# Values matmuls of latent attention: once per head pair over wide rows, with kept transposed probabilities

## Chip, cores and metric

The kernel runs on one NeuronCore of a Trainium2 chip. The metric is the device time of one execution in microseconds (us). The engines are named as in the profile: PE is TensorE's matmul stream and PEld its weight loads, DVE is VectorE, ACT is ScalarE, POOL is GpSimd and SP is SyncE.

## What is computed

Two residual layers over x of shape (1, 512, 1024) in float32. Layer 0 mixes with SSD and GLA heads, layer 1 with multi-head latent attention, and a SwiGLU FFN follows each. The change touches only layer 1's attention: 16 heads of width 64 + 32 (rotary), values of width 64, a causal softmax over 512 tokens in blocks of 128 queries.

```python
def block(i):
    start = i * ATTN_BLOCK
    ...
    s = jnp.einsum('bqhd,bkhd->bhqk', qn, k_nope) + jnp.einsum('bqhr,bkr->bhqk', qr, k_rope)
    s = s.astype(jnp.float32) * scale
    ...
    p = jax.nn.softmax(jnp.where(mask, s, -jnp.inf), axis=-1).astype(v.dtype)
    return jnp.einsum('bhqk,bkhv->bqhv', p, v)
o = lax.map(block, jnp.arange(seqlen // ATTN_BLOCK))
...
return o @ w_o
```

## The kernel before

Everything is one TensorE program in a framework that takes the instructions in program order, gives each engine its own in-order queue, and lets an instruction that comes later in the program go first at compile time when an earlier one's inputs are not expected to be ready. So the program order is a priority, and an engine at run time executes its queue strictly in the order that came out.

Dense layers hold each operand as two parts of a reduced-width type; `mm3` (lines 141 to 143) does three matmuls of 512 columns for each pair of chunks and accumulates into one of three PSUM banks named `acc`. `weight` (lines 135 and 136) loads a weight and splits it on ACT and DVE, 90 instructions ahead of its place.

Layer 1 works on groups of four heads and on pairs of heads. `project(g)` computes q, k and v of a group, token-major. `prepare(g, hp, ...)` transposes keys and queries of a pair: 4 transposes at line 821 and 8 at line 834, into the key tiles `kT` (6 of them, `NK`) and the query tiles `qT` (4). `attend(g, hp, ...)` then goes through the four query blocks b, and in each through the two heads j:

- line 848: the scores of 128 queries against (b+1) x 128 keys, into one of two PSUM banks `sco`
- line 852 (DVE): scale, mask and row minimum into `sc` (6 buffers, `SC`)
- line 854 (ACT): exp with the row sum, then line 856 (DVE) the reciprocal and line 857 (DVE) the normalisation
- line 861 (PE): b+1 transposes of 128 x 128 into one of two PSUM banks `ptr`, and line 863 (ACT) the copy into `pt` (4 buffers of 512 columns, `PT`)
- line 867 (PE): after both heads, for each key block kb up to b and each head, a matmul of 128 columns with the 64 value columns of the head as weights. Head 0 writes partitions 0 to 63 of the bank `po`, head 1 writes 64 to 127

After the four blocks `split` (lines 120 and 121) takes `po` to two parts. The main loop runs `prepare` of the next pair ahead of `attend` of this one. `project(2)` comes after pair 0, `project(3)` after pair 2, and `o_round(0)`, the dense product of the first four pairs with half of w_o, after pair 4. `o_round(1)` comes after pair 7. These dense products are what PE can do while a pair's softmax is on its way.

Of the kernel before, what the change touches and what calls it, by code (L numbers as in the profile page):

```python
# [8 lines left out]
F32 = mybir.dt.float32  # L9
F32R = mybir.dt.float32r  # L10
I32 = mybir.dt.int32
AF = mybir.ActivationFunctionType
ALU = mybir.AluOpType
# [13 lines left out]
SC, PT = 6, 4  # L27
# [4 lines left out]
# columns of the packed per-partition vectors  # L32
# [13 lines left out]
def kernel(ctx: ExitStack, tc: tile.TileContext, A, yT, stop=99):  # L46
# [11 lines left out]
    def nm(s):  # L58
        cnt[0] += 1
        return f"{s}_{cnt[0]}"  # L60
# [6 lines left out]
    def open_phase(**tags):  # L67
        """the other banks, by role"""
        if phase:
            phase["pool"].__exit__(None, None, None)  # L70
        phase["pool"] = tc.tile_pool(name=nm("pph"), bufs=1, space=PSUM)
        phase["p"] = phase["pool"].__enter__()
        phase["tags"] = tags
# [26 lines left out]
    # sel[:, c]: row 32 c is one  # L100
# [4 lines left out]
    # tri[s, l] = 1 where s <= l  # L105
# [10 lines left out]
    def split(raw_ap, th, tl, bufs, pool):  # L116
        """raw float32 [128, 512] -> exact parts hi + lo, both float32r"""
        hi = pool.tile([P, T], F32R, tag=th, name=nm(th), bufs=bufs)
        lo = pool.tile([P, T], F32R, tag=tl, name=nm(tl), bufs=bufs)
        S.copy(hi, raw_ap)  # L120
        V.tensor_tensor(lo, raw_ap, hi.bitcast(F32), ALU.subtract)
        return hi, lo

    def weight(src, kc, m):
        """src: DRAM AP [128, kc, m]; loaded and split ahead of what comes before it here"""
        with tc.high_priority(offset=AHEAD):
            return weight_now(src, kc, m)
# [17 lines left out]
    def dense(ps, w, xs):  # L145
        """ps[m, t] = sum over the chunks of w (stationary) and xs [(hi, lo)]"""
        n = len(xs)
        for k, (xh, xl) in enumerate(xs):
            mm3(ps, w[0][:, k, :], w[1][:, k, :], xh, xl, k == 0, k == n - 1)

    def rsqrt(pool, m, shape, tag, ytag=""):
        """1/sqrt(m) by bit estimate and three Newton steps; m > 0"""
        h = pool.tile(shape, I32, tag=tag + "i", name=nm(tag + "i"), bufs=1)
        y = pool.tile(shape, F32, tag=tag + ytag + "y", name=nm(tag + "y"), bufs=1)
        t = pool.tile(shape, F32, tag=tag + "t", name=nm(tag + "t"), bufs=1)
        V.tensor_scalar(h, m.bitcast(I32), 1, None, ALU.logical_shift_right)
        V.tensor_scalar(y.bitcast(I32), h, -1.0, float(0x5F3759DF), ALU.mult, ALU.add)
        for _ in range(3):
            V.tensor_tensor(t, y, y, ALU.mult)
            V.scalar_tensor_tensor(t, m, -0.5, t, ALU.mult, ALU.mult)  # L160
            V.scalar_tensor_tensor(y, t, 1.5, y, ALU.add, ALU.mult)
        return y

    def rstd(ssq, n, pool, tag):
        """ssq [128, 512]: partial sums of squares -> R [128, 512], 1/rms on every partition"""
        ps = aux()
        for c in range(4):
            E.matmul(ps[32 * c:32 * c + 32, :P], ones, ssq[:, c * P:(c + 1) * P],
                     start=True, stop=True)
        m = const.tile([P, P], F32, tag="rs_m", name=nm("rs_m"))  # L170
        V.tensor_scalar(m, ps[:, :P], 1.0 / n, EPS, ALU.mult, ALU.add)
        y = rsqrt(const, m, [P, P], "rs")
        pb = aux()
        for c in range(4):
            E.matmul(pb[:, c * P:(c + 1) * P], sel[:, c, :], y, start=True, stop=True)  # L175
        R = pool.tile([P, T], F32, tag=tag, name=nm(tag), bufs=1)
        S.copy(R, pb)
        return R

    class Norm:  # L180
        """collects the chunks of the residual: squares, and x * gain in two parts"""
# [26 lines left out]
    def tok_scalar(R):  # L208
        """R [128, 512] with equal rows -> [128 tokens, 4]"""
# [7 lines left out]
    def gate(pool, tag, ps, R, bufs):  # L217
        """silu(ps * R)"""
# [16 lines left out]
    def out_round(r, parts, nxt=None):  # L235
        """residual += (4 chunks of the mixed width) @ their rows of w_out"""
# [17 lines left out]
    with tc.tile_pool(name="gkp", bufs=1) as gkp:  # L254
        rtok = tok_scalar(R)
        # dt (rows 0..15) and the low-rank gate input (rows 32..47)
# [9 lines left out]
        # dt = softplus(dt_raw + bias), token-major [128, chunk, head]  # L266
# [41 lines left out]
        with tc.tile_pool(name="ssd", bufs=2) as sp:  # L308
# [4 lines left out]
            def conv(i, tag, bufs, bank=acc):  # L313
                """silu(causal conv) of chunk i of x|B|C, feature-major"""
# [18 lines left out]
            def group(g):  # L333
                """B and C of a group: cb[s, l] for s <= l, C feature-major, B token-major"""
# [23 lines left out]
            def core(f, xs, zg, cb, cT, btok):  # L358
                """the scan of two heads, gated by silu(z)"""
# [8 lines left out]
                # decay times cb, [s, head, chunk, l]  # L368
# [8 lines left out]
                # exp(a_cum) on the features' partitions  # L377
# [3 lines left out]
                # x * dt, token-major; and that times the decay to the chunk's end  # L381
# [10 lines left out]
                # states at the chunk starts  # L392
# [39 lines left out]
            def values(h):  # L432
                """v of a GLA head, token-major"""
# [36 lines left out]
        with tc.tile_pool(name="gla", bufs=2) as gp:  # L470
# [5 lines left out]
            # log-sigmoid of the gates, summed inside chunks of 64  # L476
# [19 lines left out]
            def inner(h, after_dense=None):  # L496
                """normalised head output times its gain; two chunks of 128 values"""
# [3 lines left out]
                # exp(g_last / 16) of each chunk  # L501
# [12 lines left out]
                # queries of a pair's second chunk, decayed from the pair's start  # L514
# [29 lines left out]
                # scores, transposed: [key, pair, query]  # L544
# [12 lines left out]
                # keys at the pairs' ends, token-major, and the states  # L557
# [109 lines left out]
    with tc.tile_pool(name="mla", bufs=2) as mp, tc.tile_pool(name="mla1", bufs=1) as m1:  # L667
        r1 = tok_scalar(R)
        # tables with the gains: rope(x) = x * ra + swapped x * rb, for q and for k
# [12 lines left out]
        # causal mask: zeros, then -1e30 where key > query in the last block  # L682
# [5 lines left out]
        # rotary key, feature-major raw  # L688
# [5 lines left out]
        # low-rank q and kv: raw (without 1/rms of the residual), times their gains, in two parts;  # L694
        # per-token factors: cf = r1 / rms(r1 * raw)
        lora, cf = {}, {}
        for who, n0, n in (("q", 0, 3), ("kv", 3, 2)):
            lora[who], ssq = [], None
            for c in range(n):
# [9 lines left out]
                sq = mp.tile([P, T], F32, tag="lsq", name=nm("lsq"))  # L709
# [15 lines left out]
        # rotary key: token-major norm and rotation, back to feature-major  # L725
        def rope(dst, src, tab, shape):
            """dst = src * ra + swapped src * rb; shape [128, 4, heads, 32]"""
# [27 lines left out]
        NK = 6  # L755
# [12 lines left out]
        def project(g):  # L768
            """q, k (normalised, rotated) and v of four heads, token-major"""
            # q of four heads  # L770
# [11 lines left out]
            # k and v of four heads  # L782
# [12 lines left out]
            # 1/rms per head  # L795
# [21 lines left out]
        def prepare(g, hp, qs, ks, v):  # L817
            """keys and queries of two heads, feature-major"""
# [21 lines left out]
        def attend(g, hp, v, kts, qts):  # L840
            """two heads: scores, softmax, values"""
            po = aux("po")
            for b in range(4):
                n = (b + 1) * P
                pts = []
                for j in range(2):
# [3 lines left out]
                    mx = mp.tile([P, 2], F32, tag="mx", name=nm("mx"), bufs=SC)  # L850
                    # -scale * (scores + mask), and its minimum
                    V.tensor_tensor_reduce(sc[:, :n], ps[:, :n], am[:, T - n:], -scale, 3e38,  # L852
                                           ALU.add, ALU.min, mx[:, 0:1])
                    S.activation(sc[:, :n], sc[:, :n], AF.Exp, bias=mx[:, 0:1], scale=-1.0,  # L854
                                 accum_out=mx[:, 1:2])
                    V.reciprocal(mx[:, 1:2], mx[:, 1:2])
                    V.tensor_scalar(sc[:, :n], sc[:, :n], mx[:, 1:2], None, ALU.mult)
                    # probabilities, transposed: [key, key block, query]
# [3 lines left out]
                    pt = mp.tile([P, T], F32, tag="pt", name=nm("pt"), bufs=PT)  # L862
                    S.copy(pt[:, :n], ps[:, :n])
                    pts.append(pt)
                for kb in range(b + 1):
                    for j in range(2):
                        E.matmul(po[64 * j:64 * j + 64, b * P:(b + 1) * P], v[:, kb, 2 * hp + j, :],  # L867
                                 pts[j][:, kb * P:(kb + 1) * P], start=(kb == 0), stop=(kb == b))
# [3 lines left out]
        def o_round(r, nxt=None):  # L872
            """residual += half of the heads @ their rows of w_o"""
# [31 lines left out]
def _layout(inp):  # L905
# [5 lines left out]
    def pieces(w, kc, m):  # L911
        """[K, M] -> [M / m, 128, kc, m]"""
        return np.ascontiguousarray(w.reshape(kc, P, -1, m).transpose(2, 1, 0, 3))
# [9 lines left out]
    # [head, half of the chunks, 128, 4 chunks, 256]  # L923
    a["w_v"] = np.ascontiguousarray(v.reshape(2, 4, P, 4, 256).transpose(3, 0, 2, 1, 4))
    a["w_g"] = pieces(g, KD, P)
    # [round of 4 chunks, pair of column chunks, 128, 4, 256]
# [7 lines left out]
    # [group of 4 heads, 128, 3, 384]  # L934
    a["w_uq"] = pieces(i["w_uq"][0], 3, 384)
    # [group, 128, 2, (k | v) x 4 heads x 64]
# [22 lines left out]
    # rotary tables, of shapes alone: [128, (cos | sin with sign), 4, 32]  # L959
# [26 lines left out]
```

## Time and profile before

| what | value |
|---|---|
| median of 3 runs | 1395.1 us (1395.07 to 1395.79) |
| span of the profiled execution | 1393.5 us |
| PE busy | 1373.1 us, 99% |
| DVE busy | 786.1 us, 56% |
| ACT busy | 559.6 us, 40% |
| attention with its dense products, by the timeline | 850 to 1010 us |
| matmuls of line 867 | 160, each recorded as two passes |

Busy time of PE counts each matmul from its start to its modelled end. Matmuls overlap in the pipeline, so what a matmul takes from the stream is the time from its start to the next start, which the timeline gives. A row of the timeline has the start, the time to the end of the last one merged in it, the engine, the line and the count.

### The profile page before, as it was taken

To read this page: it belongs to the slowest core of one execution; us is meant where nothing else is said; L and a number is where in the kernel's file an instruction comes from. 1 tells how busy PE (TensorE), PEld (TensorE's weight loads), DVE (VectorE), ACT (ScalarE), POOL (GpSimd) and SP (SyncE) were. 2 spreads that over 40 slices of the span, in tenths; PEclk is the share of its full clock that TensorE was granted. 3 is DMA by queue.
4 is the path that set the end of the run, shared out by engine and by line. 5 is a ranking of instruction groups with operands and counts; after the bars stand their busy time and mean duration, and the time that the engine had idled before them with its cause. 6 is when DMAs were issued, how large, how long until landed. Compare 5 with 4: busy or idle time off the path is not lost.

```text
span 1393.5 us, 17395 instructions
## 1 busy us (share of the span) xinstructions
PE 1373.1 (99%) x6842; PEld 1108.1 (80%) x6842; DVE 786.1 (56%) x1407; ACT 559.6 (40%) x934; POOL 9.1 (1%) x40
## 2 busy tenths in 40 slices
PE   7999999999999999999999998999999999999998
PEld 5798888687788888888888787767688888888887
DVE  7877956767667444444333459776684444443221
ACT  5665623544334232232232247774753323232111
POOL 0000000000000000000000000000000000000000
PEclk9999999999999999999999999999999999999999
DMA  5343232212233333333333321102023333333331
GB/s 174 108 148 94 68 99 77 65 57 76 65 102 91 93 104 92 105 91 94 92 101 96 99 68 49 44 31 76 1 76 106 91 103 93 92 105 102 105 109 64
DMA packets 36722, 122.21 MB, mean 88 GB/s; under 512 B 4737, under 2 KB 5761, under 8 KB 36641
## 3 DMA queue, kind: packets, MB, share of 16 engines
q1 hardware_dynamic: 35600, 120.70, 28.7%
q8 instruction: 54, 0.88, 0.3%
q10 hardware_dynamic: 1040, 0.41, 0.1%
q14 instruction: 28, 0.22, 0.1%
HBM read 118.96 MB, written 2.13 MB: 87 GB/s over the span
## 4 chain that ended last, share of the span: by engine, by line
PE 94%; DVE 4%; DMA 1%; issue 1%; ACT 1%; SPq 0%; DVEq 0%; ACTq 0%
PE acc L142 27%; PE acc L143 27%; PE acc L141 27%; PE sco L848 3%; PE po L867 2%; PE ptr L861 2%; PE st L175 1%; PE a L409 1%; DVE wlo L136 1%; PE a L579 1%; PE a L395 0%; DMA acb<-acd 0%; PE a L581 0%; PE a L413 0%; PE a L142 0%
## 5 line engine op out<-in xcount | busy, mean ns | idle before, releaser
L135 ACT CAST whi<-wraw 128x1024 fp32r<-128x1024 f32 (+2 forms) x223 | 226.6, 1017 | 576.8 <-PE acc L142 519.5
L143 PE MATMUL acc<-xh,wlo 128*128 128x512 f32 (+1 forms) x1152 | 452.5, 393 | 0.0
L142 PE MATMUL acc<-xl,whi 128*128 128x512 f32 (+1 forms) x1152 | 451.9, 392 | 0.0
L141 PE MATMUL acc<-xh,whi 128*128 128x512 f32 (+1 forms) x1152 | 451.0, 392 | 0.0
L136 DVE TENSOR_TENSOR wlo<-wraw,whi 128x1024 fp32r<-128x1024 f32 (+2 forms) x223 | 263.0, 1180 | 177.0 <-ACT whi L135 176.1
L142 PEld LDWEIGHTS acc<-xl,whi 128*128 128x128 f32 (+1 forms) x1152 | 215.7, 187 | 47.3 <-issue 3.1
L143 PEld LDWEIGHTS acc<-xh,wlo 128*128 128x128 f32 (+1 forms) x1152 | 215.7, 187 | 45.8 <-issue 1.8
L141 PEld LDWEIGHTS acc<-xh,whi 128*128 128x128 f32 (+1 forms) x1152 | 215.8, 187 | 45.1 <-issue 1.1
L141 PE MATMUL acc<-fhh,whi 128*128 128x512 f32 x288 | 112.0, 389 | 0.0
L142 PE MATMUL acc<-fhl,whi 128*128 128x512 f32 x288 | 112.0, 389 | 0.0
L143 PE MATMUL acc<-fhh,wlo 128*128 128x512 f32 x288 | 112.0, 389 | 0.0
L637 DVE TENSOR_TENSOR fu<-acc,R 128x512 f32<-128x512 f32 x44 | 30.4, 691 | 139.4 <-PE acc L143 139.4
L634 DVE TENSOR_TENSOR fg<-acc,R 128x512 f32<-128x512 f32 x44 | 30.4, 691 | 95.2 <-PE acc L143 91.3
L142 PEld LDWEIGHTS acc<-fhl,whi 128*128 128x128 f32 x288 | 54.1, 188 | 11.3
L143 PEld LDWEIGHTS acc<-fhh,wlo 128*128 128x128 f32 x288 | 54.1, 188 | 11.2
L141 PEld LDWEIGHTS acc<-fhh,whi 128*128 128x128 f32 x288 | 54.1, 188 | 11.1
L141 PE MATMUL acc<-mxh,whi 128*128 128x512 f32 x128 | 50.4, 396 | 1.3 <-ACT whi L135 1.3
L142 PE MATMUL acc<-mxl,whi 128*128 128x512 f32 x128 | 50.4, 395 | 0.0
L143 PE MATMUL acc<-mxh,wlo 128*128 128x512 f32 x128 | 50.3, 394 | 0.0
L848 PE MATMUL sco<-kT,qT 96*128 96x128 f32 (+3 forms) x128 | 45.4, 448 | 0.9 <-DVE mx L852 0.7
L852 DVE CUSTOM_DVE_ANT_0 sc<-sco,am 128x128 f32<-128x128 f32 (+3 forms) x64 | 30.8, 485 | 13.0 <-PE sco L848 12.4
L854 ACT ACTIVATE sc<-sc,mx 128x128 f32<-128x128 f32 (+3 forms) x64 | 35.8, 561 | 3.8 <-DVE mx L852 2.8
(290 smaller groups left out, 1590.6 us busy)
## 6 DMA issues: line engine op xcount, KB each, us to landing
wraw<-in_w_gate_dram SPq DMA_DIRECT2D x44, 512.0 KB, 3.6
wraw<-in_w_up_dram SPq DMA_DIRECT2D x44, 512.0 KB, 3.6
wraw<-in_w_down_dram SPq DMA_DIRECT2D x32, 512.0 KB, 3.6
wraw<-in_w_out_dram SPq DMA_DIRECT2D x16, 512.0 KB, 3.7
wraw<-in_w_xbc_dram SPq DMA_DIRECT2D x12, 512.0 KB, 3.7
wraw<-in_w_down_dram SPq DMA_DIRECT2D x16, 384.0 KB, 3.1
wraw<-in_w_z_dram SPq DMA_DIRECT2D x8, 512.0 KB, 3.6
wraw<-in_w_v_dram SPq DMA_DIRECT2D x8, 512.0 KB, 3.7
```

Source lines behind the costliest of these rows:

```text
L135: S.copy(hi[:, :kc * m], r)
L136: V.tensor_tensor(lo[:, :kc * m], r, hi.bitcast(F32)[:, :kc * m], ALU.subtract)
L141: E.matmul(out, ah, bh, start=first, stop=False)
L142: E.matmul(out, ah, bl, start=False, stop=False)
L143: E.matmul(out, al, bh, start=False, stop=last)
L634: V.tensor_tensor(g, pg, R, ALU.mult)
L637: V.tensor_tensor(u, pu, R, ALU.mult)
L848: E.matmul(ps[:, :n], qts[j][:, b * P:(b + 1) * P], kts[j][:, :n], start=True, stop=True)
L852: V.tensor_tensor_reduce(sc[:, :n], ps[:, :n], am[:, T - n:], -scale, 3e38, ALU.add, ALU.min, mx[:, 0:1])
L854: S.activation(sc[:, :n], sc[:, :n], AF.Exp, bias=mx[:, 0:1], scale=-1.0, accum_out=mx[:, 1:2])
L861: E.transpose(ps[:, kb * P:(kb + 1) * P], sc[:, kb * P:(kb + 1) * P], ident)
L867: E.matmul(po[64 * j:64 * j + 64, b * P:(b + 1) * P], v[:, kb, 2 * hp + j, :], pts[j][:, kb * P:(kb + 1) * P], start=(kb == 0), stop=(kb = ...
```

## The change

`attend` keeps the transposed probabilities of the whole pair. Each head has one tile of 13 x 128 columns (`pt`, 3 buffers over all pairs), laid out so that for each key block kb the queries from kb x 128 to 511 stand side by side. The copy at the end of a block writes b+1 pieces of 128 columns into it, 384 columns apart. After all four blocks the values matmuls run once: for each kb and head one matmul of 512, 384, 256 or 128 columns, 8 for a pair in place of 20. A manual dependency lets the first of them wait for the last copy of the pair. One reciprocal serves both heads of a block. `SC` goes from 6 to 4, `NK` from 6 to 4, and the squares of the low-rank projections share the buffers of the residual's squares. Comments and docstrings are also gone from the file.

```diff
-SC, PT = 6, 4
+SC = 4
...
-                sq = mp.tile([P, T], F32, tag="lsq", name=nm("lsq"))
+                sq = res.tile([P, T], F32, tag="sq", name=nm("lsq"), bufs=2)
...
-        NK = 6
+        NK = 4
...
         def attend(g, hp, v, kts, qts):
-            po = aux("po")
+            pts = [mp.tile([P, 13 * P], F32, tag="pt", name=nm("pt"), bufs=3) for _ in range(2)]
+            last = None
             for b in range(4):
                 n = (b + 1) * P
-                pts = []
+                mx = mp.tile([P, 2], F32, tag="mx", name=nm("mx"), bufs=SC)
+                sm = mp.tile([P, 2], F32, tag="sm", name=nm("sm"), bufs=SC)
+                scs = []
                 for j in range(2):
                     ps = aux("sco")
                     E.matmul(ps[:, :n], qts[j][:, b * P:(b + 1) * P], kts[j][:, :n], start=True, stop=True)
                     sc = mp.tile([P, T], F32, tag="sc", name=nm("sc"), bufs=SC)
-                    mx = mp.tile([P, 2], F32, tag="mx", name=nm("mx"), bufs=SC)
                     V.tensor_tensor_reduce(sc[:, :n], ps[:, :n], am[:, T - n:], -scale, 3e38,
-                                           ALU.add, ALU.min, mx[:, 0:1])
-                    S.activation(sc[:, :n], sc[:, :n], AF.Exp, bias=mx[:, 0:1], scale=-1.0,
-                                 accum_out=mx[:, 1:2])
-                    V.reciprocal(mx[:, 1:2], mx[:, 1:2])
-                    V.tensor_scalar(sc[:, :n], sc[:, :n], mx[:, 1:2], None, ALU.mult)
+                                           ALU.add, ALU.min, mx[:, j:j + 1])
+                    S.activation(sc[:, :n], sc[:, :n], AF.Exp, bias=mx[:, j:j + 1], scale=-1.0,
+                                 accum_out=sm[:, j:j + 1])
+                    scs.append(sc)
+                V.reciprocal(sm, sm)
+                for j in range(2):
+                    sc = scs[j]
+                    V.tensor_scalar(sc[:, :n], sc[:, :n], sm[:, j:j + 1], None, ALU.mult)
                     ps = aux("ptr")
                     for kb in range(b + 1):
                         E.transpose(ps[:, kb * P:(kb + 1) * P], sc[:, kb * P:(kb + 1) * P], ident)
-                    pt = mp.tile([P, T], F32, tag="pt", name=nm("pt"), bufs=PT)
-                    S.copy(pt[:, :n], ps[:, :n])
-                    pts.append(pt)
-                for kb in range(b + 1):
-                    for j in range(2):
-                        E.matmul(po[64 * j:64 * j + 64, b * P:(b + 1) * P], v[:, kb, 2 * hp + j, :],
-                                 pts[j][:, kb * P:(kb + 1) * P], start=(kb == 0), stop=(kb == b))
+                    at = 0 if b < 2 else 2 * P
+                    dst = pts[j][:, b * P - at:b * P - at + 3 * P * (b + 1)]
+                    dst = dst.rearrange("p (k q) -> p k q", q=3 * P)[:, :, at:at + P]
+                    last = S.copy(dst, ps[:, :n].rearrange("p (k q) -> p k q", q=P))
+
+            po = aux("po")
+            for kb in range(4):
+                for j in range(2):
+                    mm = E.matmul(po[64 * j:64 * j + 64, kb * P:], v[:, kb, 2 * hp + j, :],
+                                  pts[j][:, kb * T:kb * T + T - kb * P], start=(kb == 0), stop=(kb == 3))
+                    if kb == 0 and j == 0:
+                        tc.add_manual_dep(mm.ins, last.ins.name,
+                                          mybir.DependencyInfo(mybir.DependencyClass.Sync,
+                                                               mybir.DependencyReason.DATA),
+                                          reason="values of both heads in one go")
```

## Rows read from the trace of the kernel before

**Rows 1.** Page, part 1: busy us, share of span, instructions of each engine.
```profile
PE 1373.1 (99%) x6842; PEld 1108.1 (80%) x6842; DVE 786.1 (56%) x1407; ACT 559.6 (40%) x934; POOL 9.1 (1%) x40
```

**Rows 2.** Windows of attention: us, then busy us by engine, clock, DMA share, GB/s.
```profile
880.00:919.00 39.00, 38.54 (x236) 27.17 (x235) 29.55 (x95) 30.34 (x73) 0.00 (x0) 1.00 0.09 28
919.00:954.00 35.00, 34.15 (x206) 22.06 (x205) 26.55 (x91) 23.31 (x61) 0.00 (x0) 1.00 0.10 31
954.00:969.00 15.00, 15.00 (x67) 12.36 (x67) 7.12 (x9) 2.51 (x3) 0.00 (x0) 1.00 0.33 107
969.00:1010.00 41.00, 40.78 (x270) 26.31 (x269) 27.06 (x103) 29.72 (x82) 0.00 (x0) 1.00 0.05 14
```

**Rows 3.** Waits, 850 to 1010 us: who waited for whom, us, times, longest.
```profile
ACT pt L863 <- PE ptr L861: 20.8, 30, 4.6
DVE sc L852 <- PE sco L848: 12.4, 18, 2.8
PEld po L867 <- ACT pt L863: 9.4, 23, 0.8
```

**Rows 4.** Line 867 by itself: durations ns min/median/max, first and last start, form.
```profile
L867 PE MATMUL po<-pt,v x320: 272/273/324, 861.8 to 1008.9; 128*64 128x128 f32 x160
```

**Rows 5.** PE's timeline: first run of line 867, then pair 7: start, us, line, count.
```profile
861.85 0.44 PE L867 MATMUL po<-pt,v 128*64 128x128 f32 x4
...
1000.16 0.44 PE L867 MATMUL po<-pt,v 128*64 128x128 f32 x4
1000.53 0.33 PE L861 MATMUL ptr<-ident,sc 128*128 128x128 f32 x1
1000.80 0.43 PE L867 MATMUL po<-pt,v 128*64 128x128 f32 x2
1001.16 0.55 PE L861 MATMUL ptr<-ident,sc 128*128 128x128 f32 x3
1001.54 1.02 PE L848 MATMUL sco<-kT,qT 96*128 96x512 f32 x2
1002.50 0.65 PE L867 MATMUL po<-pt,v 128*64 128x128 f32 x6
1003.08 0.55 PE L861 MATMUL ptr<-ident,sc 128*128 128x128 f32 x3
1003.56 0.43 PE L867 MATMUL po<-pt,v 128*64 128x128 f32 x2
...
1008.13 1.09 PE L867 MATMUL po<-pt,v 128*64 128x128 f32 x14
1009.15 0.50 PE L143 MATMUL acc<-xh,wlo 128*128 128x512 f32 x1
1009.48 0.39 PE L141 MATMUL acc<-xh,whi 128*128 128x512 f32 x1
1009.71 0.39 PE L142 MATMUL acc<-xl,whi 128*128 128x512 f32 x1
```

**Rows 6.** Scores matmuls by form, 900 us on: count, busy us, mean ns, idle.
```profile
L848 PE MATMUL sco<-kT,qT 96*128 96x512 f32 x24 | 12.7, 610 | 0.0
L848 PE MATMUL sco<-kT,qT 96*128 96x128 f32 x20 | 3.4, 285 | 0.0
```

**Rows 7.** ACT and DVE forms of a block, 970 to 1009 us: columns as in rows 6.
```profile
L852 DVE CUSTOM_DVE_ANT_0 sc<-sco,am 128x512 f32<-128x512 f32 x6 | 4.1, 688 | 1.9 <-PE sco L848 1.9
L854 ACT ACTIVATE sc<-sc,mx 128x512 f32<-128x512 f32 x6 | 4.3, 724 | 0.5 <-DVE mx L852 0.4
L856 DVE RECIPROCAL mx<-mx 128x1 f32<-128x1 f32 x24 | 3.7, 159 | 2.1 <-ACT sc L854 1.7
L857 DVE TENSOR_SCALAR sc<-sc,mx 128x512 f32<-128x512 f32 x6 | 2.9, 486 | 0.2
L863 ACT COPY pt<-ptr 128x512 f32<-128x512 f32 x6 | 3.5, 582 | 3.1 <-PE ptr L861 3.1
L863 ACT COPY pt<-ptr 128x256 f32<-128x256 f32 x6 | 2.2, 367 | 0.7 <-PE ptr L861 0.7
```

**Rows 8.** Line 517, a copy in pieces of 64 columns: durations ns, form.
```profile
L517 ACT COPY qp<-qd x4: 405/406/407, 263.9 to 351.1; 128x256 f32<-128x256 f32 x4
```

## Prediction

> **What bounds the kernel now.** I read the page's busy shares first: PE is busy 99% of the span, DVE 56%, ACT 40% [rows 1]. But a busy PE is not a PE at its peak, so I went to the stage that the change touches. The windows show three kinds of stretch: attention mixed with dense products (880 to 954 us), a dense product alone (954 to 969), and attention with almost nothing to mix in (969 to 1010) [rows 2]. PE has work in flight all through, at full clock (1.00, the 2.4 GHz level). ACT, the next engine, is busy 29.7 of 41 us in the last stretch and DVE 27.1. The waits say who is late: ACT waits 20.8 us for the transposes, DVE 12.4 us for scores, while PE's weight loads wait 9.4 us for probability copies, 0.8 us at the longest [rows 3]. So PE is the bound here too, and what counts is the time that each matmul takes from its stream: from one start to the next, in the timeline.
>
> **What a values matmul takes today.** The 160 matmuls of line 867 are 320 passes [rows 4]. The timeline merges neighbours into runs. From start to next start, a run of 2 passes takes 0.36 us, of 4 takes 0.37, of 6 takes 0.58, of 14 takes 1.02 [rows 5]. From 6 to 14 passes it is 0.44 for 8, so 4 passes, which are one key block of both heads, cost 0.22 us: two steps of 0.109. The two heads already run side by side, which is why 4 passes cost no more than 2. A run of 2 has one head alone and pays two steps for half the work; its partner is then missing at the end of the following run.
>
> What lies beyond the steps is the price of a run. A run of 2 takes 0.36 against 0.22 of steps: 0.14. Three transposes take 0.38 between a run and a scores matmul, 0.48 between two runs [rows 5], against 3 x 0.109 = 0.33: entering a run costs 0.10 ahead of it, and the first matmul after it 0.05 more. If that is a dense matmul it takes 0.33 where the next takes 0.23 [rows 5], so 0.10. A run costs 0.29 to 0.34 us beside its steps.
>
> Between the first and the last run of those rows I counted 52 runs: 23 of 2 passes, 3 of 4, 8 of 6, one of 8, 7 of 10, 2 of 12, 8 of 14. One of 8 takes 0.71, one of 10 or 12 takes 0.80. From start to next start they sum to 23 x 0.36 + 3 x 0.37 + 8 x 0.58 + 0.71 + 9 x 0.80 + 8 x 1.02 = 30 us. Before and after them lie another 0.15 to 0.20 each, 8 to 10 us. The values cost PE 38 to 40 us.
>
> **The change on PE.** The columns stay the same: 512 + 384 + 256 + 128 are the ten blocks of 128 that a head has today. A wide matmul costs no less for each column: scores passes of 512 and 128 columns differ by 610 - 285 = 325 ns over 384 columns [rows 6], which is 0.108 us for 128. So a pair's values take 10 x 0.22 = 2.2 us as long as the heads stay side by side, plus one run's price, 0.3: 2.5 us, and 20 us for 8 pairs. PE is spared 38 to 40 less 20, about 19 us. None of it comes from width as such: 44 fewer runs at 0.29 to 0.34 are 13 to 15, and the lone steps are 5.
>
> Would wide matmuls still overlap? The trace of before has no wide one in half the columns. The nearest row is the run of 14, with six pairs of heads side by side behind one another; I take full overlap. The other end is none: 2.2 us more in each pair, 17 us. Against it stands a rule of the Trainium skill (TensorE: Matmul & The Clock Gate, The mechanism): matmuls start and end strictly in program order. If a head's two passes stood next to each other in the program, a run of 4 would need three steps by it; the measured 0.37 holds two [rows 5], so here the passes go alternately or the rule does not bind between halves. By the rule the sum would lose about 0.4 us a pair, 3.5 in all.
>
> **What the change adds elsewhere.** Copies write pieces of 128 columns. The nearest row is a copy in pieces of 64, 0.406 us against 0.367 for a plain copy of that size from PSUM [rows 7, 8]. I take 0; at the other end 64 x 0.04 = 2.6 us of ACT, which has that to spare in every window; a gain has no reason. 32 reciprocals of 0.16 go, 5 us of DVE, off the path. But the one left waits for the second head's exp and stands ahead of the first head's normalisation in DVE's queue: the first head's transposes come up to 0.7 later. Fewer `sc` buffers (two blocks in flight in place of three) and fewer `kT` make the scores of the next block wait sooner; the query tiles were already four, so `kT` I take at 0. The shared buffers for squares lie ahead of attention beside dense matmuls: 0.
>
> **The new wait.** The first values matmul of a pair waits for its last copy. Queued behind it on PE are the next pair's scores and transposes, and for these wait DVE (line 852) and ACT (lines 854, 863). From the last score on, the chain is 0.69 + 0.72 + 0.16 + 2 x 0.49 + 4 x 0.109 + 0.58 = 3.6 us [rows 7]. PE has for this time the other head's transposes (0.44), the next pair's first scores (0.44) and their transposes (0.22), and the 12 transposes that prepare the pair after (1.3): 2.4, which leaves 1.2 us open where there is no dense work. Pairs 0 to 4 have `project` and `o_round(0)` beside them: I take 0 there. Pairs 5 to 7 have little, so 3 x 1.2 = 3.6. Also, during the 2.5 us of a values run no new scores come; two score banks hold 1.4 us of DVE's work, so about 1 us is lost in each of these pairs, 2.4 or so once other queued work is counted. Together I take 6 us back. The bounds are 0 and 8 x 3.6 = 29. With less cover the same 1.2 would be 3.6 a pair.
>
> **Sum.** 19 - 6 = 13 us off the profiled 1393.5 gives a span of 1380.5. The median of the runs is 1.6 above the profiled span, so 1382.
>
> **The rivals.**
> - Latency bound: ACT and DVE set the pace once PE is relieved. For it: in the last stretch ACT is already busy 29.7 of 41 us for three pairs, PE would need about 33, and only two blocks are in flight. Against it: ACT's own waits there are for PE. If the last 41 us give nothing and the others two thirds of their 12, the gain is 5 to 8 at most once start-up is taken off: 1387 to 1390.
> - Heads no longer side by side when wide: 19 - 17 = 2 less the given back leaves 1393 to 1399; nearest to no change. Only the absent row speaks for it.
> - Slower: the wait for the last copy is not covered. Place: the end of each pair, on PE's in-order queue. Price: up to 3.6 us x 8 = 29 against 19 spared, so 1405; it decides from 19 / 8 = 2.4 us open a pair. For it: today the values matmuls themselves fill the softmax's latency in small pieces, and that filling goes. Against it: dense work stands beside five of the eight pairs, and the order may put it there.
> - The change does not do what it says: the order splits a pair's values into two runs. That would cost 8 x 0.3 = 2.4 us and lies inside the forecast's range.
>
> **How the numbers follow.** The forecast (gain of 8 to 21, 1374 to 1387) has 0.65, the latency bound 0.13, no overlap 0.10, the uncovered wait 0.12. Runs of this kernel tell 0.2%, 2.8 us, from no change. Faster are the first two, 0.78. No overlap I call the same, 0.10, and the uncovered wait slower, 0.12. The low end takes 20 spared and nothing given back: 1373 to 1375. The high end has to take in the latency bound and the near half of the no-overlap case: 1394. About 0.17 stays outside above, 0.03 below.
>
> **What would show it.** Right: line 867 has 64 matmuls in 8 runs of some 2.3 us, from start to next start, the second head starting hardly after the first; attention ends 10 to 16 us earlier, at 994 to 1000; the last stretch shrinks from 41 to about 36. Wrong: values runs of over 4 us (no overlap); PE idle of over 2 us ahead of each run, released by the copy of line 863 (uncovered wait); ACT or DVE above 90% in the last stretch (latency bound). I would also be wrong if the compiled order moved the dense products so that pairs 0 to 4 lost their cover, or if waits cost PE its clock, which is 1.00 in these windows now [rows 2].

## The result

The changed kernel takes 1386.55 us (median of 4 runs, 1385.21 to 1389.91) against 1395.44 us before: 8.9 us less, ratio 0.994 with a 95% interval of 0.9928 to 0.9953. The profiled execution has a span of 1383.5 us, 10 us below that of before. The four runs lie apart as their mean granted clock does: 1385.21 us at 1.000, 1386.35 and 1386.75 at 0.999, 1389.91 at 0.995. The forecast of 1382 had the sign and the bulk of the mechanism; 4.5 us of the expected gain did not come.

First the page of the changed kernel, part 1, beside [rows 1]:

```profile
PE 1357.4 (98%) x6650; PEld 1094.1 (79%) x6650; DVE 782.3 (57%) x1375; ACT 558.9 (40%) x934; POOL 8.0 (1%) x38
```

PE has 192 matmul records less, as 320 passes of values became 128. The values matmuls (now line 876), by themselves:

```profile
L876 PE MATMUL po<-pt,v x128: 272/432/644, 873.9 to 1001.6; 128*64 128x512 f32 x32, 128*64 128x384 f32 x32, 128*64 128x256 f32 x32, 128*64 128x128 f32 x32
```

PE's timeline around the runs of pairs 0 and 1 (start, us to the last end, line, count). They answer to the runs in [rows 5]:

```profile
873.93 2.37 PE L876 MATMUL po<-pt,v 128*64 128x512 f32 x16
876.23 0.55 PE L821 MATMUL acc<-ident,ks 128*128 128x128 f32 x3
...
895.95 2.38 PE L876 MATMUL po<-pt,v 128*64 128x512 f32 x16
898.26 0.44 PE L867 MATMUL ptr<-ident,sc 128*128 128x128 f32 x2
```

From start to next start a run takes 876.23 - 873.93 = 2.30 us. There are 8, one for each pair, and each holds all 16 passes. Behind the last one PE stands for another 0.75 us, since the first dense matmul that needs the last pair waits for its `split` (line 120):

```profile
999.51 2.37 PE L876 MATMUL po<-pt,v 128*64 128x512 f32 x16
1002.57 0.73 PE L141 MATMUL acc<-xh,whi 128*128 128x512 f32 x2 [0.69 <-ACT xh L120]
```

**Where the time went.** For each kernel I summed the timeline's start-to-start times of PE, from the first key transposes of attention (line 821) to the first matmul of the last norm (line 168). Four shares come out: the runs of values; what the matmuls just before and after a run take beyond their own step (as priced in the prediction, at most 0.10 to 0.20 a run); the other matmuls at their steps (0.109 us for 128 columns in float32, 0.23 for a dense matmul of 512); and the rest, in which PE stands open.

| kernel | us, and less than before in the same runs | runs of values | values | around them | open | sum with the other matmuls |
|---|---|---|---|---|---|---|
| before | 1395.1 | 52 | 30.2 | 8.6 | 13.3 | 183.5 |
| changed | 1386.6, 8.9 | 8 | 19.2 | 1.3 | 24.4 | 175.6 |

Values and what is around them went from 38.8 to 20.5, 18.3 us less. The open time rose by 11.1. (The 0.75 us behind the last run stand under values here; counted as open they make it 19.7 and a rise of 11.9.) The remaining 2 us of the 10 lie ahead of and behind this stretch, 1.2 and 0.9. Ahead of it the granted clock of the execution before was 0.5, the 1.2 GHz level, from 265.7 to 269.1 us, and that of the changed one 1.00. Over all experiments this stretch starts at 847.9 to 849.1 us where the clock did not fall there, and at 849.0 to 850.7 where it did. So I do not count the 1.2 us to the change. The 0.9 behind I do not explain.

The new open time has names. PE's own waits in attention of the changed kernel (who waited for whom, us, times, longest):

```profile
PE acc L141 <- ACT qT L836: 2.9, 2, 1.6
PE acc L821 <- ACT qT L836: 1.4, 3, 1.0
PE sco L853 <- DVE mx L856: 1.3, 4, 0.5
PEld po L876 <- ACT pt L871: 3.2, 8, 0.5
```

The last line is the wait of the values' weight loads (PEld) for the last copy of a pair. In the kernel before, PE has no wait of the first kind, and of the second it has

```profile
PE acc L821 <- ACT qT L836: 0.7, 2, 0.6
```

The first is not ahead of a values run but in the middle of pair 1 and of pair 3. PE's timeline in pair 1, then DVE's and ACT's:

```profile
884.14 1.12 PE L853 MATMUL sco<-kT,qT 96*128 96x512 f32 x2
886.61 0.44 PE L141 MATMUL acc<-whi,lh 128*128 128x384 f32 x1 [1.35 <-ACT qT L836]
```

```profile
883.53 0.55 DVE L856 CUSTOM_DVE_ANT_0 sc<-sco,am 128x384 f32<-128x384 f32 x1
884.00 0.08 DVE L856 DVE_READ_ACCUMULATOR2_ANT mx<- 128x1 f32 x1
884.00 1.22 DVE L807 TENSOR_TENSOR qs<-qs,hry 128x1024 f32<-128x1024 f32 x1
885.14 0.68 DVE L810 TENSOR_TENSOR rr<-qs,hry 128x512 f32<-128x512 f32 x1
885.74 1.22 DVE L814 TENSOR_TENSOR ks<-ks,hry 128x1024 f32<-128x1024 f32 x1
...
888.15 0.55 DVE L856 CUSTOM_DVE_ANT_0 sc<-sco,am 128x384 f32<-128x384 f32 x1
```

```profile
885.30 0.68 ACT L828 ACTIVATE kT<-acc,pv 64x512 f32<-64x512 f32 x1 [0.17 <-PE sco L853]
885.89 0.67 ACT L836 ACTIVATE qT<-acc,pv 96x512 f32<-96x512 f32 x1
```

DVE is at the normalisation of `project(1)` from 884.0 to 888.1, and the rest of the third block's softmax stands behind it in its queue. PE has given out the scores it has buffers for. The dense matmul that should fill the gap waits for its PSUM bank, which the query copy on ACT (line 836) frees late. In ACT's queue a key copy (line 828) stands ahead of it, and this one waited for the scores that were the last to read its key tile: pair 3 takes the tile of pair 1 when there are four. In the kernel before, with six, the key copy went without a wait at 883.75:

```profile
883.75 0.68 ACT L828 ACTIVATE kT<-acc,pv 64x512 f32<-64x512 f32 x1
886.95 0.43 PE L867 MATMUL po<-pt,v 128*64 128x128 f32 x2
888.70 0.67 ACT L836 ACTIVATE qT<-acc,pv 96x512 f32<-96x512 f32 x1
```

Pair 1's first values matmuls lay in this place there. The waits for query copies name 2.9 of the 24.4 us. The rest is in many shorter pieces that I have not put down to a cause one by one.

### The profile page after: what moved, and what is told of

Its sections match the earlier page's. It is cut to its first block, busy times and chain, and to the rows that moved or that the text cites. A ratio compares the mean times of both kernels' runs of the same rounds, so it can differ in the third digit from the quotient of the medians.

```text
span 1383.5 us, 16956 instructions
## 1 busy us (share of the span) xinstructions
PE 1357.4 (98%) x6650; PEld 1094.1 (79%) x6650; DVE 782.3 (57%) x1375; ACT 558.9 (40%) x934; POOL 8.0 (1%) x38
## 4 chain that ended last, share of the span: by engine, by line
PE 91%; DVE 6%; ACT 1%; issue 1%; DMA 1%; SPq 0%; ACTq 0%; DVEq 0%
PE acc L142 27%; PE acc L141 27%; PE acc L143 27%; PE sco L853 2%; PE ptr L867 1%; PE po L876 1%; DVE wlo L136 1%; PE st L175 1%; PE a L409 1%; PE a L579 1%; ACT whi L135 1%; PE a L395 0%; DMA x<-in_xT_dram 0%; PE a L581 0%; PE a L413 0%
```

## The experiments

Each was timed beside the kernel before, with medians of 4 to 11 runs; differences are against that, and brackets hold the 95% interval of the ratio. The median of before was 1395.1 to 1395.4 us each time, so experiments can be compared with one another.

**Fewer score buffers.**

```diff
-SC, PT = 6, 4
+SC, PT = 4, 4
```

> The kernel before with 4 score buffers (SC) in place of 6 and nothing else changed. In the changed kernel, values cost PE 18.3 us less, but the time that PE stands open between matmuls in attention rose from 13.3 to 24.4 us, so 10 of the 18 show in the span. Theory A (fewer score buffers throttle the softmax chain and take back half): this kernel is slower than before by 3 to 8 us. Theory B (the values block took the fine filling away, buffers do not matter): within 1.5 us of before. Theory C (the joint reciprocal): within 1.5 us of before.

1394.45 us, 0.7 less (0.9982 to 1.0); 50 runs, open 13.3. With narrow values four buffers cost nothing. Theory A falls for that kernel. The run shows something else as well. DVE is at the same normalisation from 888.54 us and takes no new score until 893.73, longer than in the changed kernel, and yet PE does not stand open: it has values runs of 2 and 6 passes and dense matmuls in this time. So DVE's normalisation alone does not open PE.

```profile
888.54 1.22 DVE L807 TENSOR_TENSOR qs<-qs,hry 128x1024 f32<-128x1024 f32 x1
890.08 0.65 PE L867 MATMUL po<-pt,v 128*64 128x128 f32 x6
893.73 0.69 DVE L852 CUSTOM_DVE_ANT_0 sc<-sco,am 128x512 f32<-128x512 f32 x1
```

**The joint reciprocal alone**, in the kernel before.

```diff
-                    V.reciprocal(mx[:, 1:2], mx[:, 1:2])
-                    V.tensor_scalar(sc[:, :n], sc[:, :n], mx[:, 1:2], None, ALU.mult)
...
+                V.reciprocal(sm, sm)
+                for j in range(2):
+                    sc = scs[j]
+                    V.tensor_scalar(sc[:, :n], sc[:, :n], sm[:, j:j + 1], None, ALU.mult)
```

> The kernel before with one reciprocal for both heads of a block, placed after the second head's exp as in the change; the raw rotary key shares a query buffer to make room. Theory C (the joint reciprocal locks the two heads together and lengthens the first head's chain by some 0.7 us a block): 3 to 8 us slower than before. Theories A and B: within 1.5 us of before, since 5 us of DVE work go and up to 0.7 us of chain come, both off PE's path.

1390.39 us, 4.7 less (0.9954 to 0.9979). All three theories missed this gain. The timeline says where it is from: 41 runs of values in place of 52, values and surroundings 34.5 us in place of 38.8, open 13.0. Runs of 2 passes, one head alone, fell from 23 to 12. The raw rotary key's new place came with this edit and was not timed by itself.

**Six score buffers in the changed kernel.**

```diff
-SC = 4
+SC = 6
...
-        krr = m1.tile([32, T], F32, name="krr")
+        krr = mp.tile([32, T], F32, tag="qT", name="krr", bufs=4)
...
-            rr = mp.tile([P, 16, 32], F32, tag="rr", name=nm("rr"), bufs=1)
+            rr = mp.tile([P, 16, 32], F32, tag="sq", name=nm("rr"), bufs=1)
```

> The changed kernel with 6 score buffers again; room comes from the raw rotary key in a query buffer and the rotated part in the squares' buffer. Theory A: 3 to 8 us faster than the changed kernel (1379 to 1384 us), and the open time of PE in attention falls from 24 to 16 to 20 us. Theory B: within 1.5 us of the changed kernel (1385 to 1388). Theory C: the same as B.

1383.86 us, 11.3 less than before (0.9904 to 0.993); 2.7 less than the changed kernel, though the two intervals just touch. Open 21.9 in place of 24.4. The clock is in both numbers. In the profiled execution the granted clock was 0.5, the 1.2 GHz level, from 889.3 to 892.7 us, right after PE had stood open for 1.61 us, and dense matmuls of 384 columns went at steps of 0.32 us in place of 0.17:

```profile
889.20 0.65 PE L141 MATMUL acc<-whi,lh 128*128 128x384 f32 x1 [1.61 <-ACT qT L836]
889.64 0.52 PE L142 MATMUL acc<-wlo,lh 128*128 128x384 f32 x1
889.96 0.52 PE L143 MATMUL acc<-whi,ll 128*128 128x384 f32 x1
```

Eleven of them make 1.6 us, so the open time at full clock would be some 20.3 (an estimate from these steps). The runs say the same: at a mean granted clock of 1.000 this kernel took 1381.06 and the changed one 1385.21, at 0.999 it was 1382.47 against 1386.35 and 1386.75. At a like clock the third block in flight is worth about 4 us: by the time what theory A said, by the open time just short of it. The two tiles that moved to make room came with it and were not timed by themselves.

**Without the dependency.**

```diff
-                    if kb == 0 and j == 0:
-                        tc.add_manual_dep(mm.ins, last.ins.name,
...
-                                          reason="values of both heads in one go")
```

> The changed kernel without the manual dependency, so that a wide values matmul may go as soon as its own operands are there. Theory B (PE lacks filling at the pair's end because all 16 passes wait for the last copy): 2 to 4 us faster than the changed kernel, line 876 in more than 8 runs. Theories A and C: within 1.5 us, or slower by 0.3 to 0.5 us for each further run of line 876, that is up to 4 us.

1391.04 us, 4.1 less than before (0.9958 to 0.9983), so 4.5 more than the changed kernel. The direction that theory B named is wrong, and so is the cause that I gave for the other: the runs are still 8. They are longer, though:

```profile
935.92 2.73 PE L876 MATMUL po<-pt,v 128*64 128x512 f32 x16
938.58 0.44 PE L867 MATMUL ptr<-ident,sc 128*128 128x128 f32 x2
...
950.05 2.85 PE L876 MATMUL po<-pt,v 128*64 128x512 f32 x16
952.84 0.50 PE L143 MATMUL acc<-xh,wlo 128*128 128x512 f32 x1
```

2.66 and 2.79 us in place of 2.30; in all runs values take 22.4 in place of 19.2, which is 3.2 of the 4.5 us. The starts inside a run show why, as read from the trace (ns from the start of the run):

```
changed, run at 946.50:          0, 7, 480, 487, 910, 916, 1232, 1239, 1555, 1561, ...
no dependency, run at 935.92:    0, 361, 480, 841, 909, 1231, 1271, 1554, 1593, ...
no dependency, run at 950.05:    0, 480, 488, 910, 968, 1232, 1397, 1555, 1720, ...
```

Head 1 starts 0.04 us after its copy has ended, 0.36 or 0.49 us after head 0 (the 488 in the last row), and never catches up: each half goes on at its own pace, and the run ends later by the same offset. The open time is the same (24.6).

**Separate reciprocals in the changed kernel**, the reverse of the joint reciprocal's edit.

> The changed kernel with a reciprocal for each head again, as before. In the kernel before, the joint reciprocal alone gained 4.7 us, because the runs of values matmuls fell from 52 to 41. Theory D (the joint reciprocal gains only by making fewer runs): here the runs are 8 either way, so within 1.5 us of the changed kernel (1385 to 1388). Theory E (it shortens the softmax chain or frees DVE in itself): 2 to 5 us slower, 1389 to 1391.

1382.57 us, 12.5 less than before (0.9896 to 0.9923) and 4.0 less than the changed kernel; the intervals are apart. Neither theory had this sign: the joint reciprocal costs the wide kernel 4 us. Open 20.1 in place of 24.4, and the 0.75 us behind the last values run are gone. The score matmuls' weight loads wait less for DVE to free a score bank, here in the changed kernel and then with separate reciprocals:

```profile
PEld sco L853 <- DVE mx L856: 10.0, 24, 0.7
PEld sco L850 <- DVE mx L854: 5.9, 18, 0.6
```

The joint reciprocal made the narrow kernel faster by bringing the heads into step. The wide kernel has the dependency for that, and is left with the longer chain; the waits agree with this reading, but no run tests the chain apart.

**Head by head.**

```diff
-            for kb in range(4):
-                for j in range(2):
+            for j in range(2):
+                for kb in range(4):
```

> The changed kernel with the two loops of the values matmuls exchanged: all four key blocks of head 0, then those of head 1, so that a head's passes follow one another in the program. If the halves of the array take their own matmuls independently of program order, a run stays at 2.3 us and the time within 1 us of the changed kernel. If side by side needs neighbouring passes, a run takes 4.2 to 4.4 us, PE pays 8 x 2 = 16 us more, and the kernel is 8 to 16 us slower, 1395 to 1403.

1398.84 us, 3.7 more than before (1.0014 to 1.0036), 12.3 more than the changed kernel. A run takes 878.74 - 874.88 = 3.86 us:

```profile
874.88 3.93 PE L876 MATMUL po<-pt,v 128*64 128x512 f32 x16
878.74 0.55 PE L821 MATMUL acc<-ident,ks 128*128 128x128 f32 x3
```

So full overlap needs neighbours in the program. Without them the two heads overlap for part of a run only, and the second rival comes true by 1.56 us in each of 8 runs, 12.5 in all.

**Narrow matmuls, heads in step**: the kernel before with the joint reciprocal and the dependency for each block.

```diff
-                    S.copy(pt[:, :n], ps[:, :n])
+                    last = S.copy(pt[:, :n], ps[:, :n])
...
-                        E.matmul(po[64 * j:64 * j + 64, b * P:(b + 1) * P], v[:, kb, 2 * hp + j, :],
-                                 pts[j][:, kb * P:(kb + 1) * P], start=(kb == 0), stop=(kb == b))
+                        mm = E.matmul(po[64 * j:64 * j + 64, b * P:(b + 1) * P], v[:, kb, 2 * hp + j, :],
+                                      pts[j][:, kb * P:(kb + 1) * P], start=(kb == 0), stop=(kb == b))
+                        if kb == 0 and j == 0:
+                            tc.add_manual_dep(mm.ins, last.ins.name,
...
```

> The kernel before, 20 narrow values matmuls for a pair in four places, with the joint reciprocal and a dependency that lets the first of a block wait for both heads' copies. Theory D (what counts is the number of runs and the heads in step, not width): 32 runs, values and their surroundings about 28 us of PE in place of 38.8, open time of PE stays at 13 to 16 because the fine filling stays; 8 to 11 us faster than before, 1384 to 1387, as good as the changed kernel. If width itself matters: 4 to 6 us faster, as with the joint reciprocal alone.

1381.07 us, 14.0 less than before (0.9889 to 0.9916): better than the change, with the 20 narrow matmuls of before. The blocks of pair 0 in PE's timeline (values are line 872 here):

```profile
861.03 0.44 PE L872 MATMUL po<-pt,v 128*64 128x128 f32 x4
861.40 0.44 PE L141 MATMUL acc<-whi,lh 128*128 128x384 f32 x1
...
874.07 1.10 PE L872 MATMUL po<-pt,v 128*64 128x128 f32 x16
875.10 0.50 PE L143 MATMUL acc<-whi,ll 128*128 128x512 f32 x1
```

No run begins with one head: 4 passes take 0.37, 16 take 1.03. There are 28 runs (some blocks follow one another directly), values and surroundings take 26.4, and the open time stays at 12.9. The changed kernel spends 6 us less of PE on its values than this one, and has twice that more of open time; it also has four score buffers in place of six.

**The values of a pair in two runs**, on the changed kernel with six buffers: queries 0 to 255 after the second block, 256 to 511 after the fourth.

```diff
+                if b % 2 == 0:
+                    continue
+                lo = (b - 1) * P
+                for kb in range(b + 1):
+                    q0, q1 = max(lo, kb * P), (b + 1) * P
+                    for j in range(2):
+                        mm = E.matmul(po[64 * j:64 * j + 64, q0:q1], v[:, kb, 2 * hp + j, :],
+                                      pts[j][:, kb * T + q0 - kb * P:kb * T + q1 - kb * P],
+                                      start=(kb == 0), stop=(kb == b))
...
```

> The changed kernel with 6 score buffers, the values of a pair in two runs: queries 0 to 255 after the second block, 256 to 511 after the fourth. Theory B (one block of values takes the filling away and this makes PE stand open, 21.9 us in the run with 6 score buffers): 16 runs cost 8 x 0.3 = 2.4 us more, and the open time falls by 4 to 7 us: 2 to 4 us faster than with 6 buffers, 1380 to 1382. If the open time comes from elsewhere: 2 to 3 us slower, 1386 to 1387.

1383.05 us (0.9905 to 0.9933), not told apart from one run with six buffers (1383.86). The shares moved the way that theory B says, by less: open 18.0 in place of 21.9 (20.3 without the stretch at the lower clock), values and surroundings 22.3 in place of 19.7. The exchange is even.

**Six buffers and separate reciprocals.**

> The changed kernel with 6 score buffers and a reciprocal for each head. Separate reciprocals alone gained 4.0 us over the changed kernel, six buffers alone 2.7. Theory F (two different waits, both given back: the first head's chain behind the second head's exp, and the third block in flight): gains add, 5 to 7 us under the changed kernel, 1380 to 1382, with PE open for 17 to 19 us. Theory G (both ease the same wait): no better than separate reciprocals alone, 1382 to 1383, PE open for 20.

1382.01 us, 13.2 less than before (0.9887 to 0.9917), the same as separate reciprocals alone (1382.57). Open 18.9, with the granted clock at 0.5 from 854.8 to 858.2 us in this execution. By the time theory G holds and the gains do not add; the open time lies in the range of theory F. So that the two edits ease mostly the same wait is likely and not shown.

**The dependency alone**, in the kernel before.

> The kernel before with one change: the first values matmul of a block waits for the copies of both heads. Reciprocals stay separate. If the joint reciprocal always costs chain and only helped in the kernel before by bringing the heads into step: faster than with both (1381.1), 1376 to 1380. If with narrow blocks it costs nothing, since PE has other filling: the same, 1380 to 1382. If the dependency alone does not bring the heads together: 1385 to 1390, with more than 32 runs.

1384.11 us, 11.1 less (0.9909 to 0.9934); 31 runs, values and surroundings 27.2, open 14.3. The dependency by itself brings the heads together. The joint reciprocal on top gave 3.0 more, with intervals that overlap. In the profiles the stretch of attention differs by 1.6 us (172.3 and 170.7); the rest lies ahead of it, where the granted clock was 0.5 from 265.1 to 271.9 us in this execution and not in the other. In this kernel the joint reciprocal does not cost what it costs the wide one.

**Two runs, six buffers, separate reciprocals.**

> The changed kernel with 6 score buffers, the values of a pair in two runs, and a reciprocal for each head. Two runs with the joint reciprocal gave 1383.1. If the chain of the first head still costs 4 us there: 1378 to 1380. If the second run has already covered it: 1382 to 1384.

1379.09 us, 16.1 less than before (0.9871 to 0.9898) and 4.0 less than two runs with the joint reciprocal: by its median the fastest kernel of this study, though its interval and that of narrow matmuls in step overlap, and 7.5 below the changed one. PE stands open for 14.8, with 22.3 for values and surroundings. In pair 1 the first of the two runs (line 874) lies about where the changed kernel stood open:

```profile
885.40 1.02 PE L851 MATMUL sco<-kT,qT 96*128 96x512 f32 x2
886.26 0.27 PE L863 MATMUL ptr<-ident,sc 128*128 128x128 f32 x1
886.47 0.87 PE L874 MATMUL po<-pt,v 128*64 128x256 f32 x8
887.27 0.44 PE L863 MATMUL ptr<-ident,sc 128*128 128x128 f32 x2
```

**The side edits**, in the kernel before: `NK` at 4 and the shared buffers for squares.

> The kernel before with the two side edits of the change alone: 4 key tiles (NK) in place of 6, and the low-rank squares in the residual's buffers. All theories: within 1.5 us of before, since the query tiles already hold a pair's preparation back to two pairs, and the squares lie beside dense matmuls. If it is slower by 2 us or more, part of the open time belongs to these edits.

1392.42 us, 2.9 less (0.9972 to 0.999). Expected was no difference. The shares show 48 runs in place of 52, values and surroundings 36.7, open 12.3. The edit touches no values matmul; it shifts the compiled order a little, and with it the number of runs. The key copies on ACT wait for scores here too (0.47 us at 886.0), but PE never waits for a bank that a query copy holds. In the wide kernel the four key tiles were not timed by themselves.

Put in a row, the kernels with narrow values show one line:

| narrow kernel | runs | values and surroundings | open | less than before, us |
|---|---|---|---|---|
| before | 52 | 38.8 | 13.3 | 0 |
| 4 score buffers | 50 | 38.0 | 13.3 | 0.7 |
| 4 key tiles | 48 | 36.7 | 12.3 | 2.9 |
| joint reciprocal | 41 | 34.5 | 13.0 | 4.7 |
| dependency | 31 | 27.2 | 14.3 | 11.1 |
| both | 28 | 26.4 | 12.9 | 14.0 |

## Why the prediction was right, and where it was off

**What bounds the kernel.** Right. With the open time steady at 12 to 14 us, the narrow kernels gain what their values runs lose, within 1.6 us. The time of 1386.55 lies at the upper end of the forecast's 1374 to 1387: the range held by its width, and the sum was 4.5 us off.

**The price of a run and the sum on PE.** Right: 38 to 40 to start from, 38.8 measured; 20 after, 20.5 measured; 19 spared, 18.3 measured. The two heads do stay side by side at 512 columns. That width brings nothing but fewer runs shows in the steps: the four narrow runs of a pair in step take 0.37 + 0.59 + 0.81 + 1.03 = 2.80 us, the wide one 2.30, and 0.50 for three more runs is 0.17 each, near the 0.14 that a run was priced at beyond its own steps. Which kernel is faster is another matter. Narrow in step beats the changed kernel (1381.07 against 1386.55), but with separate reciprocals, and six score buffers on both sides, the wide one is ahead by its median (1382.01 against 1384.11, intervals that overlap). The copies in pieces were rightly taken at 0: 0.589 us for 512 columns in place of 0.582, 0.372 in place of 0.367 for 256.

**The rule on program order.** The sum had taken full overlap over a loss of 3.5 us, and the runs of 2.30 us bear that out. The head-by-head run tests the rule directly. Head 1's first pass (its 512 columns tell it apart) starts 1.560 us into the run, ahead of three passes of head 0 that started at 1.770, 1.986 and 2.095 us, although all of head 0 stands first in the compiled program. The Trainium skill (TensorE: Matmul & The Clock Gate, The mechanism) has matmuls start strictly in program order; between the two halves of the array this trace shows otherwise, though only over a few passes, and the measurement decides. That an engine executes its queue strictly in the order that came out, as the section on the kernel before has it, does not hold for PE's two halves.

**What was given back.** This is the term that was mis-sized: 6 us forecast, 11.1 measured, inside the bounds of 0 and 29. Its place was wrong too. The step that failed says that pairs 0 to 4 have dense work beside them, so nothing is lost there. By stretches the open time went from 2.8 to 6.9 us in the 38 us that hold pairs 1 and 2, from 3.0 to 6.3 in the next 34, and from 1.7 to 5.3 after the dense product. The last 3.6 were forecast as 6; the first two, 7.4 together, as 0. Where the trace names a cause, the cover was there in the program and could not start: its PSUM banks were held by query copies that ACT makes late, while DVE was at the next group's normalisation. These waits are 2.9 us in the changed kernel, 3.2 with six buffers, 1.9 with separate reciprocals, 1.2 with two runs, and none with six buffers and separate reciprocals or in any narrow kernel; the open time falls in roughly this order. They account for a part of the 11.1. The experiments say more on which edits it belongs to: with reciprocals separate, six score buffers and two runs in place of one, the open time is 14.8 in place of 24.4, so 9.6 of the 11.1 go back to these three together. No run had another number of these banks, so which waits make up the rest stays open. The four key tiles, taken at 0, have a part in it: with them a key copy waits in ACT's queue ahead of the query copy. I had counted cover in microseconds of work and not asked what buffers it needs.

**The joint reciprocal** was put down as 5 us of DVE off the path, with 0.7 us of chain and no cost of its own. In the wide kernel it costs 4.0 us. That taking it out gives 1382.6, the forecast, is a coincidence: the forecast took 6 us back for other reasons. **Four score buffers** were named and not priced: 2.7 us with wide values by the medians, about 4 at a like clock, none with narrow.

**The wait for the last copy**, the price of the slower rival, was small: PE's weight loads waited 3.2 us for it over 8 runs. The dependency proved useful, because it starts the heads together. The time lies 0.45 us below the latency-bound rival's 1387 to 1390; that rival's sign, ACT or DVE above 90% in the last stretch, did not come about (28.5 and 25.2 of 39.5 us, 72 and 64%).

**The signs.** The 8 runs of 2.3 us came. The end of attention did not: the last values run ends at 1001.8 us, not at 994 to 1000. Nor did the last stretch shrink to 36: from the end of the dense product to the end of the last run it is 39.5 us, against 39.9 before, because 27 dense matmuls lie in it now and 11 lay in it before. At 0.23 us each the 16 more are 3.7 us, and without them it is 35.8. The granted clock was 1.00 in all windows of attention of the changed kernel's profiled execution. But the fear that waits cost PE its clock was not idle: it fell to 0.5 right after a wait of 1.6 us for a query copy with six buffers (889.3 us) and head by head (932.2 us), while the same wait at 925.6 us in the changed kernel left it at 1.00.

What remains open is why a joint reciprocal costs narrow blocks in step nothing when it costs the wide kernel 4 us; fewer runs, 28 against 31, is argued and not shown.

## What to carry over

When two half-array matmuls can run side by side, check in the start times that they begin together and stand next to each other in the program; a lone half costs as much as a pair, and each switch into and out of half-array matmuls has its own price (0.3 us here). Collecting such matmuls into one late block saves switches and takes away filling, so price both, and try the middle (two blocks here). Work counted as cover needs its buffers free at that moment: look at who holds them.

## What was not expected of the hardware

Two streams of matmuls in the two halves of the array keep their own pace once started: an offset of 0.36 or 0.49 us at the start of a run was still there at its end, and the run was longer by it (2.66 and 2.79 against 2.30 us). Heads that stand apart in the program overlap only by a few passes (3.86 us a run in place of 2.30). A wait of 1.6 us can be followed by a stretch at half the granted clock: in the two executions where it was, eleven dense matmuls of 384 columns went at 0.32 us in place of 0.17 and nine of 512 at 0.43 in place of 0.23, about as much again as the wait.
